# Contrast adjustment on one core: 64 KB rows in three kept buffers, two hardware DMA queues, tiles moved as every second row, sum shared by two engines

## The chip, the cores and the metric

The kernel runs on one core of a Trainium2 chip. The metric is device time in microseconds (us) of one execution; figures are medians of several executions, with their range. A profile covers one execution, and its span is about 2 us shorter than the metric. Runs are marked fast or slow by their time alone. The experiments ran in three batches on different chips, each beside the kernel before, whose medians there were 240.29, 240.23 and 239.88 us; differences of half a microsecond between batches are therefore not resolved.

A packet is one record of the DMA trace, here nearly always one contiguous run of a transfer (also called a row below; 1536 records of 64 KB in the changed kernel), on one of 16 DMA engines. In the trace each transfer ends with 16 packets of 4 bytes, called completion writes below (416 for the 26 transfers of the kernel before), and has 16 semaphore updates; it has landed at the last of these.

## The reference

```python
# x: 16 x 3 x 512 x 512 float32, factor = 1.5
def reference(x, factor):
    mean = np.mean(x, axis=(2, 3), keepdims=True)
    return np.clip(mean + factor * (x - mean), 0, 1).astype(np.float32)
```

There are 48 images of 1 MB. Each must be read in full before its mean is known, and then every pixel is rescaled and clipped. 50.33 MB are read and 50.33 MB written, whatever the kernel does.

## The kernel before

A tile is four images, 4 MB: 32 partitions for each image, 32 KB in each partition, one DMA in and one out. Eleven such tiles are followed by two of two images, so that the last one is small. Five buffers rotate. VectorE sums each partition, a matmul with a block matrix adds the partitions of an image, ScalarE applies `relu(1.5 x + bias)` and VectorE takes the minimum with 1.

```python
TILE_IMGS = [4] * 11 + [2, 2]
X_BUFS = 5
STORE_ENGINE = "gpsimd"
# ... (pools, block matrices, addresses cut)
    for i, N in enumerate(TILE_IMGS):
        FREE = n_pix * N // P                       # 8192 columns for four images
        nc.sync.dma_start(out=xt, in_=src)          # P rows of FREE elements
        nc.vector.tensor_reduce(out=rsum, in_=xt, axis=mybir.AxisListType.X, op=mybir.AluOpType.add)
        nc.tensor.matmul(pbias, blockw[N], rsum, start=True, stop=True)
        nc.scalar.copy(out=bias, in_=pbias)
        nc.scalar.activation(out=xt, in_=xt, func=mybir.ActivationFunctionType.Relu, bias=bias, scale=factor)
        nc.vector.tensor_scalar(out=xt, in0=xt, scalar1=1.0, scalar2=None, op0=mybir.AluOpType.min)
        store_eng.dma_start(out=dst, in_=xt)        # gpsimd: the software queue
```

Of the kernel before, what the change touches and what calls it, by code (L numbers as in the profile page):

```python
# [1 line left out]

# [4 lines left out]


TILE_IMGS = [4] * 11 + [2, 2]  # L10
X_BUFS = 5
STORE_ENGINE = "gpsimd"


@with_exitstack
def kernel(
    ctx: ExitStack,
    tc: tile.TileContext,
    x: bass.AP,
    factor: float,  # L20
    out: bass.AP,
):
    nc = tc.nc
    P = 128

    B, C, H, W = x.shape
    n_img = B * C
    n_pix = H * W

    factor = float(factor)  # L30
    f32 = mybir.dt.float32

    assert sum(TILE_IMGS) == n_img
    NMAX = max(TILE_IMGS)

    x_f = x.rearrange("b c h w -> (b c h w)")
    out_f = out.rearrange("b c h w -> (b c h w)")

    wconst = (1.0 - factor) / float(n_pix)

    consts = ctx.enter_context(tc.tile_pool(name="consts", bufs=1))
    blockw = {}
    for N in sorted(set(TILE_IMGS)):
        wt = consts.tile([P, P], f32, name=f"blockw{N}")
        PPI = P // N
        if N == 1:
            nc.gpsimd.memset(wt, wconst)
        else:
            nc.gpsimd.memset(wt, 0.0)  # L49
            for b in range(N):  # L50
                nc.gpsimd.memset(wt[b * PPI : (b + 1) * PPI, b * PPI : (b + 1) * PPI], wconst)  # L51
        blockw[N] = wt

    xpool = ctx.enter_context(tc.tile_pool(name="xpool", bufs=X_BUFS))
    rpool = ctx.enter_context(tc.tile_pool(name="rpool", bufs=12))
    bpool = ctx.enter_context(tc.tile_pool(name="bpool", bufs=12))
    psum = ctx.enter_context(tc.tile_pool(name="psum", bufs=8, space=bass.MemoryType.PSUM))

    if STORE_ENGINE == "sync":
        store_eng = nc.sync  # L60
    elif STORE_ENGINE == "act":
        store_eng = nc.scalar
    else:
        store_eng = nc.gpsimd

    pix_off = 0
    for i, N in enumerate(TILE_IMGS):
        FREE = n_pix * N // P
        npix_tile = n_pix * N

        xt = xpool.tile([P, NMAX * n_pix // P], f32, name="xt")[:, :FREE]
        src = bass.AP(tensor=x_f.tensor, offset=pix_off, ap=[[FREE, P], [1, FREE]])
        dst = bass.AP(tensor=out_f.tensor, offset=pix_off, ap=[[FREE, P], [1, FREE]])
        nc.sync.dma_start(out=xt, in_=src)  # L74

        rsum = rpool.tile([P, 1], f32)
        nc.vector.tensor_reduce(  # L77
            out=rsum,
            in_=xt,
            axis=mybir.AxisListType.X,  # L80
            op=mybir.AluOpType.add,
        )

        pbias = psum.tile([P, 1], f32)
        nc.tensor.matmul(pbias, blockw[N], rsum, start=True, stop=True)  # L85

        bias = bpool.tile([P, 1], f32)
        nc.scalar.copy(out=bias, in_=pbias)  # L88

        nc.scalar.activation(  # L90
            out=xt,
            in_=xt,
            func=mybir.ActivationFunctionType.Relu,
            bias=bias,
            scale=factor,
        )
        nc.vector.tensor_scalar(  # L97
            out=xt,
            in0=xt,
            scalar1=1.0,  # L100
            scalar2=None,
            op0=mybir.AluOpType.min,
        )
        store_eng.dma_start(out=dst, in_=xt)  # L104

        pix_off += npix_tile


# [1 line left out]
_INS = ['x', 'factor']  # L110
_OUTS = [((16, 3, 512, 512), 'float32')]
#: Inputs that are plain numbers.
_NUMBERS = {'factor': 1.5}


# [26 lines left out]
```

## Time and profile before

| | before |
|---|---|
| time | 240.01 us (239.79 to 240.62) when predicted; 240.19 us with later runs |
| span of the profile | 238.6 us |
| HBM traffic over the span | 422 GB/s |
| busy: VectorE (DVE), ScalarE (ACT) | 66%, 37% |

These are lines of the page of the kernel before. A digit is the busy share of one fortieth of the span in tenths; the GB/s line has the traffic in the same slices.

```profile
span 238.6 us, 238 instructions
...
DVE  0088999999599079459629909917945979742300
ACT  2002966472906601900920650470190095406000
...
DMA  7999999999999999999999999999999999999995
GB/s 269 434 439 439 439 439 352 439 434 439 439 439 439 439 434 434 423 428 412 423 439 439 434 439 439 439 439 439 434 428 426 426 404 428 431 434 439 428 434 214
```

The DMA strip is full from the second slice to the last but one, while both compute engines have gaps. The next view gives the same by stretches, 42 to 196 us and the three stretches of the end: length, then busy us (instructions) of TensorE's matmuls (PE), its weight loads (PEld), VectorE, ScalarE and POOL, then clock, DMA share, GB/s.

```profile
42.00:196.00 154.00, 5.18 (x18) 4.50 (x18) 110.74 (x18) 63.07 (x18) 4.80 (x9) 1.00 1.01 434
196.00:217.00 21.00, 1.12 (x4) 1.01 (x4) 15.47 (x4) 6.39 (x4) 2.99 (x2) 1.00 0.99 421
217.00:225.00 8.00, 0.00 (x0) 0.00 (x0) 2.29 (x1) 3.83 (x2) 0.53 (x1) 1.00 1.05 455
```

From 217 to 225 us the last small tile is still being computed, and the DMA engines are full nonetheless, with stores that had queued up. The groups of instructions price the compute (busy us, mean ns of one, idle before and what ended it):

```profile
L77 DVE TENSOR_REDUCE rsum<-xt 128x1 f32<-128x8192 f32 (+1 forms) x13 | 104.4, 8029 | 61.7 <-DMA xt<-in_x_dram 61.7
L90 ACT ACTIVATE xt<-xt,bias 128x8192 f32<-128x8192 f32 (+1 forms) x13 | 85.8, 6598 | 0.4
L97 DVE TENSOR_SCALAR xt<-xt 128x8192 f32<-128x8192 f32 (+1 forms) x13 | 53.2, 4091 | 5.0 <-ACT xt L90 5.0
```

VectorE waits for loads, 61.7 us in all, not the other way round.

### The profile page before, as it was taken

Reading aid. Unit: us, or ns where it says so; the run is one execution under the profiler, and the core shown is the slowest. Engines: PE = TensorE matmul, PEld = TensorE weight load, DVE = VectorE, ACT = ScalarE, POOL = GpSimd, SP = SyncE. Lnnn points to the kernel's source line nnn. Section 1 sums busy time; section 2 is a strip of 40 time slices with the busy share of each in tenths; the row PEclk is TensorE's granted clock in tenths of the full one; section 3 lists DMA queues with packets and bytes.
Section 4 is the critical chain, followed back from the end, with each engine's and each line's share of the span. In section 5 each row is a group of like instructions: output and inputs, shape, how many; then the busy total and the mean of one; then the engine's idle time right before and its main releaser. Section 6 shows DMA issues by size and latency. Waiting matters only on the chain.

```text
span 238.6 us, 238 instructions
## 1 busy us (share of the span) xinstructions
PE 7.4 (3%) x26; PEld 6.5 (3%) x26; DVE 156.5 (66%) x26; ACT 89.1 (37%) x27; POOL 10.3 (4%) x25
## 2 busy tenths in 40 slices
PE   0000000000000000000000000000000000000000
PEld 0000000000000000000000000000000000000000
DVE  0088999999599079459629909917945979742300
ACT  2002966472906601900920650470190095406000
POOL 2000001000000000000000000000000000500000
DMA  7999999999999999999999999999999999999995
GB/s 269 434 439 439 439 439 352 439 434 439 439 439 439 439 434 434 423 428 412 423 439 439 434 439 439 439 439 439 434 428 426 426 404 428 431 434 439 428 434 214
DMA packets 3744, 100.66 MB, mean 422 GB/s; under 512 B 416, under 2 KB 416, under 8 KB 416
## 3 DMA queue, kind: packets, MB, share of 16 engines
q1 hardware_dynamic: 1872, 50.33, 49.4%
q0 software_dynamic: 1872, 50.33, 49.0%
HBM read 50.33 MB, written 50.33 MB: 422 GB/s over the span
## 4 chain that ended last, share of the span: by engine, by line
issue 38%; DMA 35%; DVE 18%; POOL 2%; POOLq 0%; SPq 0%
DMA xt<-in_x_dram 19%; DMA out_dram<-xt 16%; DVE rsum L77 11%; DVE xt L97 7%; POOL out_dram L104 2%; POOLq L137 0%; SPq L74 0%; POOLq L104 0%
## 5 line engine op out<-in xcount | busy, mean ns | idle before, releaser
L77 DVE TENSOR_REDUCE rsum<-xt 128x1 f32<-128x8192 f32 (+1 forms) x13 | 104.4, 8029 | 61.7 <-DMA xt<-in_x_dram 61.7
L90 ACT ACTIVATE xt<-xt,bias 128x8192 f32<-128x8192 f32 (+1 forms) x13 | 85.8, 6598 | 0.4
L97 DVE TENSOR_SCALAR xt<-xt 128x8192 f32<-128x8192 f32 (+1 forms) x13 | 53.2, 4091 | 5.0 <-ACT xt L90 5.0
L88 ACT COPY bias<-pbias 128x1 f32<-128x1 f32 x13 | 2.1, 160 | 130.6 <-PE pbias L85 130.6
L104 POOL DMA_DIRECT2D out_dram<-xt x13 | 9.0, 692 | 213.0 <-DVE xt L97 212.8
L85 PE MATMUL pbias<-rsum,blockw 128*128 128x1 f32 x26 | 7.4, 355 | 209.5 <-DVE rsum L77 209.5
L85 PEld LDWEIGHTS pbias<-rsum,blockw 128*128 128x128 f32 x26 | 6.5, 311 | 210.3 <-DVE rsum L77 107.1
L88 ACT ACT_TABLE_LOAD x1 | 1.3, 1283 | 0.8 <-PEq L123 0.8
L51 POOL MEMSET blockw<- 32x32 f32 (+1 forms) x6 | 0.8, 128 | 0.2
L49 POOL MEMSET blockw<- 128x128 f32 x2 | 0.3, 205 | 0.3 <-POOLq L123 0.3
L123 POOL MEMSET const-float32-0.0<- 128x1 f32 x1 | 0.1, 104 | 0.2 <-issue 0.2
L123 POOL MEMSET const-bfloat16-1.0<- 128x1 bf16 x1 | 0.1, 113 | 0.0
L123 POOL MEMSET const-uint8-127<- 128x1 uint8 x1 | 0.1, 113 | 0.0
L123 POOL MEMSET const-float32-1.0<- 128x1 f32 x1 | 0.1, 110 | 0.0
## 6 DMA issues: line engine op xcount, KB each, us to landing
xt<-in_x_dram SPq DMA_DIRECT2D x11, 4096.0 KB, 24.6
out_dram<-xt POOLq DMA_DIRECT2D x11, 4096.0 KB, 36.0
xt<-in_x_dram SPq DMA_DIRECT2D x2, 2048.0 KB, 19.5
out_dram<-xt POOLq DMA_DIRECT2D x2, 2048.0 KB, 19.1
```

Of the source, the lines that this page charges most:

```text
L49: nc.gpsimd.memset(wt, 0.0)
L51: nc.gpsimd.memset(wt[b * PPI : (b + 1) * PPI, b * PPI : (b + 1) * PPI], wconst)
L77: nc.vector.tensor_reduce(out=rsum, in_=xt, axis=mybir.AxisListType.X, op=mybir.AluOpType.add,)
L85: nc.tensor.matmul(pbias, blockw[N], rsum, start=True, stop=True)
L88: nc.scalar.copy(out=bias, in_=pbias)
L90: nc.scalar.activation(out=xt, in_=xt, func=mybir.ActivationFunctionType.Relu, bias=bias, scale=factor,)
L97: nc.vector.tensor_scalar(out=xt, in0=xt, scalar1=1.0, scalar2=None, op0=mybir.AluOpType.min,)
L104: store_eng.dma_start(out=dst, in_=xt)
L123: nc = _bacc.Bacc("TRN2", target_bir_lowering=False, num_devices=1)
```

## The change

Its intent is fewer and longer DMA runs (64 KB in each partition), stores on a hardware queue, and a shorter sum because ScalarE takes half of the columns. A tile is now 8 MB, eight images of 16 partitions; there are six tiles in three buffers. Each tile moves in two DMAs, even rows and odd rows, so that each DMA touches partitions all over the array and a reload can begin when half of the old tile is stored.

```diff
-TILE_IMGS = [4] * 11 + [2, 2]
-X_BUFS = 5
-STORE_ENGINE = "gpsimd"
+ROW = 16384        # elements: 64 KB
+BUFS = 3
+HALF = ROW // 2
+CHUNK = 4096
+JUNK = 2048
+PARTS = 2
 ...
+    def dram(ap, t, r):
+        return bass.AP(tensor=ap.tensor, offset=(t * P + r) * ROW, ap=[[PARTS * ROW, P // PARTS], [1, ROW]])
+    def load(t):
+        for r in range(PARTS):
+            nc.sync.dma_start(out=xt[r::PARTS, :], in_=dram(x_f, t, r))
+    def compute(t):
+        nc.vector.tensor_reduce(out=sums[:, 0:1], in_=xt[:, 0:HALF], ...)
+        for j in range(n_act):                       # 4 pieces of the other half
+            a = HALF + j * JUNK
+            nc.scalar.activation(out=junk, in_=xt[:, a : a + JUNK], func=Act.Copy, accum_out=sums[:, 1 + j : 2 + j])
+        for j in range(1 + n_act):
+            nc.tensor.matmul(pbias, blockw, sums[:, j : j + 1], start=j == 0, stop=j == n_act)
+        nc.scalar.copy(out=bias, in_=pbias)
+        for c in range(0, ROW, CHUNK):
+            part = xt[:, c : c + CHUNK]
+            nc.scalar.activation(out=part, in_=part, func=Act.Relu, bias=bias, scale=factor)
+            nc.vector.tensor_scalar(out=part, in0=part, scalar1=1.0, scalar2=None, op0=Alu.min)
+    def store(t):
+        for r in range(PARTS):
+            nc.scalar.dma_start(out=dram(out_f, t, r), in_=xt[r::PARTS, :])
+    with tc.manual_schedule():
+        for t in range(min(BUFS, n_tiles)): load(t)
+        for t in range(n_tiles):
+            compute(t); store(t)
+            if t + BUFS < n_tiles: load(t + BUFS)
```

(Set-up lines, small tiles and the block matrix are cut.)

More of the change, by code (lines that the diff above doesn't have):

```diff
@@ L5 @@
 import concourse.tile as tile
-from concourse import bass_utils, mybir
+from concourse import mybir
 from concourse._compat import with_exitstack
-TILE_IMGS = [4] * 11 + [2, 2]
-X_BUFS = 5
-STORE_ENGINE = "gpsimd"
+P = 128
+ROW = 16384
[4 more added lines that the diff above has]
+PARTS = 2
 @with_exitstack
@@ L23 @@
     nc = tc.nc
-    P = 128
+    f32 = mybir.dt.float32
+    Alu = mybir.AluOpType
+    Act = mybir.ActivationFunctionType
     B, C, H, W = x.shape
-    n_img = B * C
-    n_pix = H * W
+    n_img, n_pix = B * C, H * W
+    ppi = n_pix // ROW
+    per_tile = P // ppi
+    n_tiles = n_img // per_tile
+    assert ppi * ROW == n_pix and per_tile * n_tiles == n_img
     factor = float(factor)
-    f32 = mybir.dt.float32
-    assert sum(TILE_IMGS) == n_img
-    NMAX = max(TILE_IMGS)
+    wconst = (1.0 - factor) / float(n_pix)
@@ L36 @@
     x_f = x.rearrange("b c h w -> (b c h w)")
     out_f = out.rearrange("b c h w -> (b c h w)")
-    wconst = (1.0 - factor) / float(n_pix)
+    def dram(ap, t, r):
+        return bass.AP(
+            tensor=ap.tensor, offset=(t * P + r) * ROW, ap=[[PARTS * ROW, P // PARTS], [1, ROW]]
+        )
     consts = ctx.enter_context(tc.tile_pool(name="consts", bufs=1))
-    blockw = {}
-    for N in sorted(set(TILE_IMGS)):
-        wt = consts.tile([P, P], f32, name=f"blockw{N}")
-        PPI = P // N
-        if N == 1:
-            nc.gpsimd.memset(wt, wconst)
-        else:
-            nc.gpsimd.memset(wt, 0.0)
-            for b in range(N):
-                nc.gpsimd.memset(wt[b * PPI : (b + 1) * PPI, b * PPI : (b + 1) * PPI], wconst)
-        blockw[N] = wt
@@ L54 @@
-    xpool = ctx.enter_context(tc.tile_pool(name="xpool", bufs=X_BUFS))
-    rpool = ctx.enter_context(tc.tile_pool(name="rpool", bufs=12))
-    bpool = ctx.enter_context(tc.tile_pool(name="bpool", bufs=12))
-    psum = ctx.enter_context(tc.tile_pool(name="psum", bufs=8, space=bass.MemoryType.PSUM))
-    if STORE_ENGINE == "sync":
-        store_eng = nc.sync
-    elif STORE_ENGINE == "act":
-        store_eng = nc.scalar
-    else:
-        store_eng = nc.gpsimd
-    pix_off = 0
-    for i, N in enumerate(TILE_IMGS):
-        FREE = n_pix * N // P
-        npix_tile = n_pix * N
-        xt = xpool.tile([P, NMAX * n_pix // P], f32, name="xt")[:, :FREE]
-        src = bass.AP(tensor=x_f.tensor, offset=pix_off, ap=[[FREE, P], [1, FREE]])
-        dst = bass.AP(tensor=out_f.tensor, offset=pix_off, ap=[[FREE, P], [1, FREE]])
-        nc.sync.dma_start(out=xt, in_=src)
-        rsum = rpool.tile([P, 1], f32)
+    xpool = ctx.enter_context(tc.tile_pool(name="xpool", bufs=1))
@@ new lines @@
+    jpool = ctx.enter_context(tc.tile_pool(name="jpool", bufs=1))
+    rpool = ctx.enter_context(tc.tile_pool(name="rpool", bufs=2))
+    bpool = ctx.enter_context(tc.tile_pool(name="bpool", bufs=2))
+    psum = ctx.enter_context(tc.tile_pool(name="psum", bufs=2, space=bass.MemoryType.PSUM))
+    blockw = consts.tile([P, P], f32, name="blockw")
+    nc.gpsimd.memset(blockw, 0.0)
+    for a in range(0, P, 2 * ppi):
+        mid, end = a + ppi, a + 2 * ppi
+        nc.gpsimd.memset(blockw[a:end, mid:end], wconst)
+        nc.gpsimd.memset(blockw[a:mid, mid:end], 0.0)
+        nc.gpsimd.memset(blockw[a:mid, a:mid], wconst)
@@ L77 @@
+    bufs = [xpool.tile([P, ROW], f32, name=f"x{b}") for b in range(BUFS)]
+    def load(t):
+        xt = bufs[t % BUFS]
+        for r in range(PARTS):
+            nc.sync.dma_start(out=xt[r::PARTS, :], in_=dram(x_f, t, r))
+    def compute(t):
+        xt = bufs[t % BUFS]
+        n_act = (ROW - HALF) // JUNK
+        sums = rpool.tile([P, 1 + n_act], f32, name="sums")
         nc.vector.tensor_reduce(
-            out=rsum,
-            in_=xt,
-            axis=mybir.AxisListType.X,
-            op=mybir.AluOpType.add,
-        )
@@ L84 @@
-        pbias = psum.tile([P, 1], f32)
-        nc.tensor.matmul(pbias, blockw[N], rsum, start=True, stop=True)
-        bias = bpool.tile([P, 1], f32)
-        nc.scalar.copy(out=bias, in_=pbias)
-        nc.scalar.activation(
-            out=xt,
-            in_=xt,
-            func=mybir.ActivationFunctionType.Relu,
-            bias=bias,
-            scale=factor,
-        )
-        nc.vector.tensor_scalar(
-            out=xt,
-            in0=xt,
-            scalar1=1.0,
-            scalar2=None,
-            op0=mybir.AluOpType.min,
-        )
@@ L104 @@
-        store_eng.dma_start(out=dst, in_=xt)
-        pix_off += npix_tile
+            out=sums[:, 0:1], in_=xt[:, 0:HALF], axis=mybir.AxisListType.X, op=Alu.add
+        )
+        for j in range(n_act):
+            junk = jpool.tile([P, JUNK], f32, name="junk")
+            a = HALF + j * JUNK
+            nc.scalar.activation(
+                out=junk, in_=xt[:, a : a + JUNK], func=Act.Copy, accum_out=sums[:, 1 + j : 2 + j]
+            )
+        pbias = psum.tile([P, 1], f32, name="pbias")
@@ new lines, in compute @@
+        for j in range(1 + n_act):
+            nc.tensor.matmul(pbias, blockw, sums[:, j : j + 1], start=j == 0, stop=j == n_act)
+        bias = bpool.tile([P, 1], f32, name="bias")
+        nc.scalar.copy(out=bias, in_=pbias)
+        for c in range(0, ROW, CHUNK):
+            part = xt[:, c : c + CHUNK]
+            nc.scalar.activation(out=part, in_=part, func=Act.Relu, bias=bias, scale=factor)
+            nc.vector.tensor_scalar(out=part, in0=part, scalar1=1.0, scalar2=None, op0=Alu.min)
@@ L110 @@
+    def store(t):
+        xt = bufs[t % BUFS]
+        for r in range(PARTS):
+            nc.scalar.dma_start(out=dram(out_f, t, r), in_=xt[r::PARTS, :])
+    with tc.manual_schedule():
+        for t in range(min(BUFS, n_tiles)):
+            load(t)
+        for t in range(n_tiles):
+            compute(t)
+            store(t)
+            if t + BUFS < n_tiles:
+                load(t + BUFS)
 _INS = ['x', 'factor']
```

## The prediction

The sum in this text came to a span of 239 to 240.5 us, about 241.5 us of time. The author's guess gave one chance in five to 255 to 300 us with rows in steps of two.

> **What bounds the kernel now.** The DMA engines. The busy-tenths strip shows DMA at 9 in every slice but the first and last, at 434 to 439 GB/s in most; the windows view gives 434 GB/s and a full DMA share from 62 to 196 us. In the trace's DMA records every full packet is one 32 KB row and mostly takes 1.213 us on one of 16 engines. 100.66 MB is 3072 such rows, so 3072 x 1.213 / 16 = 232.9 us of the 238.6 us span is transfer that no schedule removes. Left are about 6 us: start (first packet at 1.75 us, first 4 MB tile landed at 13.0 instead of 11.4), small dips, and 1.8 us from the last packet to the end. DVE (66% busy) and ACT (37%) are not the bound.
>
> **What changes.** Bytes stay the same. Rows double to 64 KB: a 16 KB row took 0.611 us against 1.213 for 32 KB, so about 0.009 us per packet is fixed; 1536 fewer packets over 16 engines save 0.9 us. Stores leave the software queue of POOL (4.7 us from the first store's issue to its first packet; a hardware load needs 1.0 us). With queues nearly always full, that saves under 1 us.
>
> Added: tiles are 8 MB, six of them, in three buffers. Compute of one tile, from the trace's durations: DVE sum of 8192 columns 8.7 us, with ACT's four 2048-column sums (about 2.0 us each by its slope) beside it; ten fp32 matmul passes instead of two, about 2.5 to 3 us; four Relu pieces of 3.65 us; last min 2.3 us: about 28.5 us landing to store. Each tile needs 38.6 us of transfer, so in the middle compute hides. A half's reload waits only for that half's store.
>
> **The ends decide.** The start is hidden: 24 MB of loads keep DMA busy until about 58 us, while the first tile lands at 22.7 us and its store comes at about 51.5 us. At the end, before has two 2 MB tiles; now the last 8 MB tile lands at about 189 us, computes until about 217, then has 19.3 us of stores. Stores still queued when it lands cover some 23 to 27 us of that, so DMA idles for about 2 to 6 us. A sum with equal shares for both queues gives a span of 239 to 240.5 us, about 241.5 us of time: saved packets against the tail hole.
>
> [...]
>
> **Predicted: 241.5 us, range 237.5 to 253.** Faster by over 2%: 0.03; within 2%: 0.67; slower: 0.30.
>
> **What would show it.** Right: 64 KB packets at about 2.42 us; 434 GB/s from 6 to 200 us; a DMA dip near 210 to 217 us; the chain ending in last-tile compute (sum, matmul, Relu, min) followed by about 20 us of store. Wrong: packets longer than 2.6 us or fewer GB/s in the first 50 us[...]; holes in the middle (three buffers too few[...]); compute per tile over 33 us.

## The result, and the profile after

| | before | after |
|---|---|---|
| time | 240.19 us (239.79 to 240.62) | 246.95 us (245.16 to 249.87) |
| span of the profile | 238.6 us | 244.7 us |
| GB/s over the span | 422 | 411 |

The ratio is 1.0264, with a 95% interval of 1.0221 to 1.0307: slower by 2.6%. A ratio is the mean time of one kernel's fast runs over that of the other's of the same rounds, so it is not quite the ratio of the medians. One of the four runs (249.87 us) counted as slow; the median of the three fast ones is 246.51 us, which is also the profiled run. Differences below are taken from this 246.51.

The same lines of the page for the changed kernel:

```profile
span 244.7 us, 338 instructions
...
DVE  0002925597157933730853550490761192563000
ACT  0002979939895879910859930486970195990000
...
DMA  9797989997979798999998999999999999834995
GB/s 343 343 514 343 514 375 482 407 450 343 514 343 514 343 503 353 503 396 461 418 441 353 503 396 461 418 439 428 439 418 439 428 428 471 386 171 171 514 439 246
```

The see-saw between 343 and 514 is how whole 64 KB packets fall into slices of 6 us; the trace's DMA records, spread over each packet's duration, give 430 to 434 GB/s in nearly every stretch up to 218 us. What is real is the "34" near the end of the DMA strip, with ScalarE at "99" just above it. By stretches:

```profile
60.00:190.00 130.00, 9.14 (x40) 8.79 (x40) 62.67 (x19) 83.42 (x46) 0.00 (x0) 1.00 0.99 428
196.00:217.00 21.00, 2.29 (x10) 2.21 (x10) 12.07 (x4) 17.87 (x13) 0.00 (x0) 1.00 0.95 412
217.00:225.00 8.00, 0.00 (x0) 0.00 (x0) 4.51 (x2) 3.48 (x1) 0.00 (x0) 1.00 0.31 131
```

From 217 to 225 us the DMA share is 0.31, where it was 1.05 before. The chain of waits that ended last shows who holds it up; columns are start, duration and what:

```profile
167.35 27.25 DMA x<-in_x_dram
...
194.72 8.70 DVE sums L82
203.41 0.04 issue
203.46 2.31 PE pbias L93 x10
205.76 0.02 issue
205.79 0.17 ACT bias L95
...
209.59 10.90 ACT x L98 x3
220.52 2.29 DVE x L99
```

The last tile lands at 194.60 us. Its sum, ten matmul passes (the page counts 60 for the 30 matmuls), four clipped pieces and the last minimum run one after another until 222.8 us, and only then can either of its stores be issued. The groups confirm the prices of the single steps (VectorE's sum of half the columns 8.683 us, the pieces 3.696 and 2.294 us, ScalarE's partial sums 1.909 us plus 0.186 us each for reading the accumulator):

```profile
L98 ACT ACTIVATE x<-x,bias 128x4096 f32<-128x4096 f32 x24 | 87.0, 3696 | 0.2
L99 DVE TENSOR_SCALAR x<-x 128x4096 f32<-128x4096 f32 x24 | 55.1, 2294 | 61.5 <-ACT x L98 61.5
L82 DVE TENSOR_REDUCE sums<-x 128x1 f32<-128x8192 f32 x6 | 52.1, 8683 | 54.4 <-DMA x<-in_x_dram 54.4
L88 ACT ACTIVATE junk<-x 128x2048 f32<-128x2048 f32 x24 | 45.8, 1909 | 46.0 <-DMA x<-in_x_dram 38.1
```

To see where the hole comes from, the trace's DMA records were grouped by transfer (this is a calculation from the trace, not a view of the profile; us from the span's start):

```
                          issued   first packet   last packet ends   landed
before  first store        36.06       40.72
before  first reload       61.44       64.94
before  a middle reload   157.19      161.84          180.15         181.72
before  last load         192.35      196.71          210.13         211.71
after   first store        51.35       56.80           72.06
after   first reload       72.53       76.36           94.51          97.27
after   last load         167.35      173.92          191.82         194.60
after   last store but 2  184.71      207.14          218.39         218.74
after   last tile's store 222.84      223.98
after   its second half   223.36      233.71          243.55         243.90
```

The end of the changed kernel adds up exactly: landing 194.60 + 28.24 of compute + 1.14 to the first packet + 19.57 of store + 1.18 to the end = 244.73 us. The stores of earlier tiles had run out at 218.39, so no packet was in flight for 5.59 us. Divided by 16 engines, the packets' times sum to 234.6 us after and 234.5 us before, so nearly all of the 6.1 us by which the span grew is time in which engines stood idle (10.2 us of the span after, 4.1 before). So the loss is mainly that hole, and bytes did not get slower: a 64 KB packet took 2.418 us and a 32 KB packet 1.213 us in the median, 2.444 and 1.221 us in the mean. The saving of 0.9 us that was expected of longer rows does not show.

### The profile page after: what moved, and what is told of

It is laid out like the page before. It is cut to its first block, busy times and chain, and to the rows that moved or that the text cites. A ratio compares the mean times of both kernels' runs of the same rounds, so it can differ in the third digit from the quotient of the medians.

```text
span 244.7 us, 338 instructions
## 1 busy us (share of the span) xinstructions
PE 13.7 (6%) x60; PEld 13.2 (5%) x60; DVE 107.0 (44%) x30; ACT 137.3 (56%) x79; POOL 1.4 (1%) x17
## 4 chain that ended last, share of the span: by engine, by line
DMA 37%; ACT 21%; DVE 16%; another core or an unknown queue 8%; issue 5%; PE 4%; SPq 0%; DVEq 0%
ACT x L98 21%; DMA x<-in_x_dram 20%; DMA out_dram<-x 17%; DVE sums L82 14%; PE pbias L93 4%; DVE x L99 2%; SPq L76 0%; ACT bias L95 0%; DVEq L82 0%
## 5 line engine op out<-in xcount | busy, mean ns | idle before, releaser
L98 ACT ACTIVATE x<-x,bias 128x4096 f32<-128x4096 f32 x24 | 87.0, 3696 | 0.2
L99 DVE TENSOR_SCALAR x<-x 128x4096 f32<-128x4096 f32 x24 | 55.1, 2294 | 61.5 <-ACT x L98 61.5
L82 DVE TENSOR_REDUCE sums<-x 128x1 f32<-128x8192 f32 x6 | 52.1, 8683 | 54.4 <-DMA x<-in_x_dram 54.4
L88 ACT ACTIVATE junk<-x 128x2048 f32<-128x2048 f32 x24 | 45.8, 1909 | 46.0 <-DMA x<-in_x_dram 38.1
L93 PE MATMUL pbias<-sums,blockw 128*128 128x1 f32 x60 | 13.7, 354 | 192.0 <-DVE sums L82 192.0
L93 PEld LDWEIGHTS pbias<-sums,blockw 128*128 128x128 f32 x60 | 13.2, 329 | 192.4 <-DVE sums L82 160.5
L88 ACT ACT_TABLE_LOAD x1 | 1.3, 1283 | 23.1 <-DMA x<-in_x_dram 23.1
L95 ACT COPY bias<-pbias 128x1 f32<-128x1 f32 x6 | 1.0, 159 | 13.8 <-PE pbias L93 13.8
L88 ACT ACTIVATION_READ_ACCUMULATOR junk<-x 128x1 f32 x24 | 4.5, 186 | 0.0
L67 POOL MEMSET blockw<- 16x16 f32 x4 | 0.4, 104 | 0.2
L68 POOL MEMSET blockw<- 16x16 f32 x4 | 0.4, 104 | 0.0
```

What stands on the lines that cost most here:

```text
L67: nc.gpsimd.memset(blockw[a:mid, mid:end], 0.0)
L68: nc.gpsimd.memset(blockw[a:mid, a:mid], wconst)
L82: nc.vector.tensor_reduce(out=sums[:, 0:1], in_=xt[:, 0:HALF], axis=mybir.AxisListType.X, op=Alu.add)
L88: nc.scalar.activation(out=junk, in_=xt[:, a : a + JUNK], func=Act.Copy, accum_out=sums[:, 1 + j : 2 + j])
L93: nc.tensor.matmul(pbias, blockw, sums[:, j : j + 1], start=j == 0, stop=j == n_act)
L98: nc.scalar.activation(out=part, in_=part, func=Act.Relu, bias=bias, scale=factor)
```

## The experiments

Theory: the DMA engines are full throughout, so compute counts only where the store queue runs dry, behind the last tile; and it runs dry there because splitting tiles by rows makes the sum wait for both DMAs and both stores wait for the last column. Rivals: compute in series slows the middle through three buffers; 64 KB runs, 64 partitions in steps of two, or the hardware queue cost something of their own.

### Longer compute in the middle, and at the end

Two kernels change one number: in chosen tiles VectorE sums all columns alone.

```diff
+        cut = ROW if t in (2, 3, 4) else HALF     # first kernel;  t in (5,) in the second
-        n_act = (ROW - HALF) // JUNK
+        n_act = (ROW - cut) // JUNK
-            ... in_=xt[:, 0:HALF]
+            ... in_=xt[:, 0:cut]
```

> The changed kernel, but in tiles 2, 3 and 4 VectorE sums all 16384 columns alone (17.4 us for the sum instead of 8.7, and one matmul instead of five, so compute of these tiles is about 7 us longer). Theory (only the last tile's compute lies on the critical path, because the DMA engines are full until 218 us): no change, 247 us within 1 us. Rival (compute per tile, 28 us in series, delays every store and so every reload in three buffers): three tiles at 7 us, so up to 20 us slower, 255 to 267 us.

> The same lengthening in tile 5, the last, alone. Theory: the hole before the last store grows by the full 7 us, from 5.6 to about 12.5 us, and the time becomes about 253.5 us (252.5 to 255). Rival (the loss is spread over the middle): one tile of six, about 1 us slower.

Lengthening three middle tiles gave 246.86 us (245.66 to 246.98), ratio 1.0267 against the 1.0264 of the changed kernel: nothing. Lengthening the last tile alone gave 253.62 us (251.72 to 254.67), 7.1 us more than the changed kernel. Its timeline shows the sum on one engine and the store that follows:

```profile
193.10 17.22 DVE L83 TENSOR_REDUCE sums<-x 128x1 f32<-128x16384 f32 x1 [10.55 <-DMA x<-in_x_dram]
...
228.06 1.13 ACTq L105 DMA_DIRECT2D out_dram<-x  x2
```

The time without any packet grew from 5.6 to 12.1 us (217.14 to 229.20). In the first kernel the middle tiles did get longer: tile 3 needed 35.1 us from landing to store instead of 28.2. The same lengthening costs nothing in three tiles of the middle and its full size in the last. The rival of a slowed middle falls.

### Column halves instead of every second row

```diff
-            offset=(t * P + r) * ROW, ap=[[PARTS * ROW, P // PARTS], [1, ROW]]
+            offset=t * P * ROW + r * (ROW // PARTS), ap=[[ROW, P], [1, ROW // PARTS]]
-        ... xt[r::PARTS, :]
+        ... xt[:, r * ROW // PARTS : (r + 1) * ROW // PARTS]
```

> The changed kernel with every tile moved in two DMAs of column halves (128 partitions, 32 KB runs) instead of every second row (64 partitions, 64 KB runs); order and bytes per DMA as before. Theory (a landing and a first packet wait behind one or more packets of the other queue): the landing lag in mixed stretches falls from 2.8 to about 1.6 us, the last load ends some 2 us earlier in the store queue's favour, time about 245 us (243.5 to 246). [...] theory: 1.213 us per 32 KB, the same. Rival (long rows save time): slower than 247 us.

It gave 239.54 us (239.48 to 239.68), ratio 0.9974 (0.9956 to 0.9992). That beats the changed kernel by 2.8% and is a quarter of a per cent under the kernel before, which counts as the same; it misses the expectation, which had looked only at waiting behind packets. The timeline of its last tile shows what had been overlooked:

```profile
182.57 8.68 DVE L82 TENSOR_REDUCE sums<-x 128x1 f32<-128x8192 f32 x1
...
195.54 1.91 ACT L88 ACTIVATE junk<-x 128x2048 f32<-128x2048 f32 x1 [15.21 <-DMA x<-in_x_dram]
...
214.18 0.34 ACTq L104 DMA_DIRECT2D out_dram<-x  x1
...
221.38 0.34 ACTq L104 DMA_DIRECT2D out_dram<-x  x1
```

VectorE sums the first half of the columns at 182.6 us, before the second half has landed at 195.52; and the first half is stored at 214.2 us, 7.2 us ahead of the second, although both stores stand after all the work in program order (ScalarE's sequencer issued the DMA at 214.18 us, while its engine was in the third piece until 215.42). The first store needs 18.7 us from the landing instead of 28.2. The hole is gone:

```profile
217.00:225.00 8.00, 0.00 (x0) 0.00 (x0) 3.04 (x2) 2.02 (x1) 0.00 (x0) 1.00 0.99 426
```

But this kernel differs from the changed one in three things at once: the DMAs themselves (32 KB runs, 128 partitions each instead of 64), early sum, early store. The next two separate them.

### Column halves made late again

Both move column halves. In the first, the order of pieces makes the first store wait for the last piece, and VectorE's half of the sum straddles both DMAs. The second has the order of pieces alone.

```diff
-        for c in range(0, ROW, CHUNK):
+        for c in (2 * CHUNK, 3 * CHUNK, 0, CHUNK):                 # both kernels
-            ... in_=xt[:, 0:HALF]
+            ... in_=xt[:, HALF // 2 : HALF // 2 + HALF]            # all-late kernel only
-            a = HALF + j * JUNK
+            a = j * JUNK if j < n_act // 2 else HALF + j * JUNK    # all-late kernel only
```

> Column halves in 32 KB runs as in the third experiment, but made as late as in the changed kernel: VectorE sums the middle half of the columns, so it needs both DMAs, and the pieces are clipped in the order third, fourth, first, second, so that the first store waits for the last piece. From the last landing to the first store 27.5 to 28.5 us as in the changed kernel. Theory A (the gain of columns came from starting the sum and the store early): the hole before the last store returns, 3 to 6 us, time 243.5 to 246. Theory B (the gain came from 32 KB instead of 64 KB runs, or from 128 instead of 64 partitions): time stays at 239.5 to 240.5.

> Column halves, sum started early (VectorE on the half that lands first), but both stores late by the order of pieces. Landing of the second half to first store about 25.8 us. Theory A: about 2.5 us better than the all-late run, 241 to 243, so that the early store accounts for the rest down to 239.5. Theory B: 239.5 to 240.5, no different from the columns run.

All late: 244.61 us (244.41 to 245.54), as its theory A had it, and the stretch without a packet is back, from 217.67 to 222.93. Early sum alone: 243.64 us (243.23 to 244.17), slightly above the 241 to 243 expected, with 2.8 us without a packet (218.70 to 221.54). Early store as well, the run above: 239.54 us. So of the 7.0 us between row halves and column halves, about 4.1 come from the store that starts early, about 1.0 from the sum that starts early, and the rest, about 1.9 by the medians, from moving columns at all; no run separates the shorter runs from the 128 partitions there. The profiled spans put that last part at 0.9 us (244.7 to 243.8), so its size is not well known. Nor do the parts add up in any order: the early store alone, with everything else by rows, brings 5.6 us (next experiment). A piece of the last part can be seen: while the other queue was busy, a load landed 2.8 us after its last packet in the changed kernel (191.82 to 194.60), 1.6 us in the kernels with 32 KB runs (192.19 to 193.84 here, 180.15 to 181.72 before), and 0.3 to 0.5 us with no other queue busy.

### Only the last tile's store by columns

```diff
+            if t == n_tiles - 1:
+                cols = bass.AP(tensor=out_f.tensor, offset=t * P * ROW + r * HALF, ap=[[ROW, P], [1, HALF]])
+                nc.scalar.dma_start(out=cols, in_=xt[:, r * HALF : (r + 1) * HALF])
+            else:
-            nc.scalar.dma_start(out=dram(out_f, t, r), in_=xt[r::PARTS, :])
+                nc.scalar.dma_start(out=dram(out_f, t, r), in_=xt[r::PARTS, :])
```

> The changed kernel in everything but the store of the last tile, which leaves as two column halves instead of every second row. The first of them needs only the first two of four clipped pieces and can be issued about 7 us earlier, at about 215.7 us, before the earlier stores have drained at 218.4. Theory (the whole loss beside the kernel before is the hole at 218 to 224 us): the hole of 5.6 us closes, time 241 to 241.8. Rival (64 KB rows, or hardware queues, cost in the middle too): 244 or more.

It gave 240.90 us (239.36 to 241.13), ratio 1.0012 (0.9973 to 1.0052), the same as before. Of its two stores the first was issued at 216.05 instead of 222.84 us, and no moment without a packet was left after the start. Ten of twelve stores and all loads still move as 64 KB rows of every second partition, on two hardware queues. So those parts cost at most about 1.3 us together beside the kernel before (the interval's upper end, net of whatever the change gains), and one pair of DMA instructions at the end accounts for 5.6 us (246.51 to 240.90), the length of the hole. The strip of this run for comparison:

```profile
span 239.3 us, 339 instructions
...
DMA  9898989897999898989898989898989999998994
```

### Contiguous halves of the rows

```diff
-            offset=(t * P + r) * ROW, ap=[[PARTS * ROW, P // PARTS], [1, ROW]]
+            offset=(t * P + r * P // PARTS) * ROW, ap=[[ROW, P // PARTS], [1, ROW]]
-        ... xt[r::PARTS, :]
+        ... xt[r * P // PARTS : (r + 1) * P // PARTS, :]
```

> The changed kernel with rows 0 to 63 in the first DMA and 64 to 127 in the second, instead of every second row. [...] packets of 64 KB take about 4.8 us in the load-only start, about 217 GB/s, the first tile lands at about 41 us instead of 23 and the time passes 300 us. If the step of two is irrelevant: 2.42 us per packet, 247 us.

It took 390.94 us (380.93 to 391.88). The first tile landed at 44.1 us instead of 23.1, and the load-only start runs at half the rate:

```profile
GB/s 215 215 215 215 215 215 188 168 289 323 256 323 330 242 336 316 256 336 309 269 323 310 303 309 303 309 323 323 316 303 336 343 242 135 47 121 215 222 209 108
```

So the partitions of a single DMA mattered by a factor of two here: 64 neighbouring ones moved at 215 GB/s in this start, 64 in steps of two at 434 GB/s. Why was not shown. The edit also makes each DMA's rows neighbours in HBM, but that is not the reason: one DMA of 128 neighbouring rows (next experiment) ran its load-only start at 434 GB/s. What the prediction feared, slow packets with rows in steps of two, is another pattern, and no run produced it.

### One DMA for a tile

```diff
-PARTS = 2
+PARTS = 1
```

> The changed kernel with one DMA of 128 rows per tile instead of two of every second row. A reload then waits for the store of a whole tile, about 9 to 10 us longer, once per buffer turn; the load queue falls behind and the last tile lands some 2 us later, at about 196 us, with fewer stores left behind it. Theory: 247.5 to 249.5. If the reload by halves was worth nothing: 246.9[...].

It gave 254.73 us (254.10 to 255.95), 5 us worse than the expectation's upper end. A reload then waits for a whole tile's store: the load queue was empty from 66.9 to 86.1 us, the last tile landed at 202.9 us, and 12.5 us passed without a packet (219.43 to 231.92). The strip shows the hole as wide:

```profile
DMA  8979999799989998989979999899899998303994
```

The direction was right and the size was not. The first reload was issued 9.3 us later than in the changed kernel (81.84 against 72.53), as expected, and its first packet waited 4.2 us against 3.8; but of this delay 8.3 us reached the last landing (202.87 against 194.60), where the expectation had let 2 through. While the load queue was empty the stores ran alone, so fewer of them were left to cover the end. Splitting the tile was worth 8.2 us (254.73 against 246.51).

### The stores' queue

```diff
-            nc.scalar.dma_start(out=dram(out_f, t, r), ...)       # changed kernel
+            nc.gpsimd.dma_start(out=dram(out_f, t, r), ...)

-STORE_ENGINE = "gpsimd"                                           # kernel before
+STORE_ENGINE = "act"
```

> The changed kernel with its stores back on the software queue of POOL. In both kernels the first store's first packet came about 5 us after its issue (4.7 software, 5.4 hardware), with the load queue busy, so the kind of queue should matter little; at the end of the kernel, with nothing in flight, the hardware store needed 1.1 us[...]. Theory: 246.5 to 248.5. If the hardware queue itself was the gain or the loss of the change: off by over 2 us either way.

> The kernel before with its stores on the hardware queue of ACT, the one part of the change that costs nothing elsewhere. The DMA engines have under 1.5 us of idle to give back beside the start, so theory: 239.3 to 240.5, at most 0.4 per cent better. If it is over 1 us slower, ACT is held up by waiting for VectorE before each store.

The changed kernel with software-queue stores took 248.52 us (246.72 to 249.24), at the upper edge of the expectation; its profiled span was 244.9 us against 244.7 for the changed kernel. By the ratios (1.0333 against 1.0264, intervals overlapping) the software queue is slower by something between nothing and 3 us; more is not resolved. The expectation allowed the software queue an extra microsecond in the hole; that is not in the trace: the last tile's store needed 1.11 us from issue to first packet, against 1.14 on the hardware queue.

The kernel before with stores on ScalarE's queue took 271.57 us (270.83 to 272.38), 13% slower and far outside the expectation. The queue is not the reason. Before, the scheduler orders the instructions, and it put two or three stores in a row into ScalarE's stream, each of which waits for VectorE's minimum; ScalarE stands still behind them. From the view of waits (who waited for whom: us in total, times, longest):

```profile
ACT bias L88 <- PE pbias L85: 101.9, 6, 29.0
ACT bias L88 <- DVE xt L97: 60.0, 4, 23.0
```

The second line is such a stop; it does not occur before, when POOL did this waiting (212.8 us for VectorE's minimum). Three stretches without a packet, of 2.5, 9.4 and 13.3 us, each end with a store that ScalarE issued late (at 133.59, 198.67 and 247.81 us). This is read from the one trace; no run gave this kernel a fixed order. So, as far as these runs show, the hardware queue and the fixed program order of the change belong together; taking the first without the second costs 31 us.

### Four column quarters

The column kernel with `PARTS = 4`, that is 16 KB runs.

> The changed kernel with four column quarters per tile (128 partitions, 16 KB runs). Starts sum and stores earlier still, and lets the landing lag fall to about 1 us (one packet of 0.61 us plus 0.4), but the packets cost 1.222 instead of 1.213 us per 32 KB, 1.7 us over the kernel. With no hole left to close: 240.5 to 242, between 1 and 2 us slower than two column halves.

It gave 240.41 us (240.07 to 241.11), ratio 1.0017 (0.9983 to 1.0051), just under the 240.5 to 242 expected. A 16 KB packet took 0.611 us, the rate fell from 433 to 431 GB/s, and there was no hole left to close. Loads landed 0.97 us after their last packet beside a busy queue, as expected. Two halves have the lowest time found, though the two intervals touch.

## Why the prediction was right or wrong

The measured 246.95 us lies inside the stated range of 237.5 to 253, and 5.5 us above the 241.5 that was named. The mechanism named, a hole at the end behind the last tile's compute, is what came; its size and so the sign of the result were missed, and it was the width of the range that held the number. The outcome held likeliest, within 2%, did not come; the kernel is 2.6% slower, to which 0.30 had been given.

- **What bounds the kernel:** right. Three middle tiles lengthened by about 7 us each changed nothing, and a kernel without a hole returns to 239.5 to 241 us.
- **"The ends decide":** right, and shown twice: the last tile's compute counts in full, and storing that one tile by columns gives the time back. Compute from landing to store was put at about 28.5 us and was 28.2.
- **"The last 8 MB tile lands at about 189 us":** this is the step that failed. It landed at 194.6, and everything behind it is added to that. The prediction's text has 1.0 us from issue to first packet, as for the very first load, when nothing else was in flight, and no lag of a landing. In a queue that has run empty beside a busy one it was 5.4 us for the first store and 3.8 us for the first reload, which began at 76.4 us. The landing of the last load came 2.8 us after its last packet. The trace before showed both: 3.5 us for the first reload, 4.7 for the first store (which the prediction put down to the software queue) and 1.6 us of landing lag. A third part is the mean packet, where the prediction counted every row at the median: the 1232 packets done when the last load ended took 2.449 us in the mean, not 2.418, which is 2.4 us over 16 engines. An estimate puts the three together: a replay of the two queues with equal shares (in the changed kernel loads and stores each moved 214 GB/s from 80 to 140 us), a small calculation and not a run, lands the last tile at 187.7 us with 1.0 us to a first packet, a lag of 0.35 us and packets of 2.418 us, and at 194.9 us with 5.45 and 3.83 us, 2.78 us and 2.444 us as measured. No run changed one of the three alone.
- **"DMA idles for about 2 to 6 us":** it was 5.6 us, inside the stretch but at its far end; the span of 239 to 240.5 us fits only its near end. The dip came at 218.4 to 224.0 us, not at 210 to 217.
- **"Save 0.9 us" by 64 KB rows:** not seen; packets summed to 234.6 us against 234.5, and the mean 64 KB packet took about twice the mean 32 KB one (2.444 and 1.221 us).
- **The hardware queue "saves under 1 us":** not contradicted. The runs leave anything from nothing to 3 us in the changed kernel.
- **The risk with rows in steps of two, one chance in five of 255 to 300 us:** it did not come about; 64 rows in steps of two ran at 434 GB/s. Contiguous rows were slow (391 us), which is another pattern.
- **What it did not see at all:** the split by rows is what makes the tail long. A row split gives no column to start on early. The prediction treated 28.5 us as the price of an 8 MB tile, when the same tile in column halves needs 18.7 us to its first store.

The landing lag is explained by the traces. It fits one packet of the other queue at three sizes (0.36 + 2.42 = 2.78 us, 0.36 + 1.21 = 1.57 us, 0.36 + 0.61 = 0.97 us), and the queues take turns in the traces: of the 1064 data packets that start from 100 to 180 us in the kernel before, 932 start where packets of the other queue alone end (12 ns apart at most), and 391 of 528 in the changed kernel. The records of the changed kernel's last load show the waiting itself: all 16 completion writes start 2.41 us after a last data packet of the load (from 188.42 to 190.83 us for the first, from 191.82 to 194.23 us for the last), each at the moment at which a packet of the store queue ends. For the last load of the kernel before it is 1.21 us (from 208.88 to 210.09 us for the first), again up to the end of a store packet. For the very first load, with no store in flight, they follow their data at once, within 0.01 us in the changed kernel.

Left open: why a first packet takes 3.5 to 5.5 us beside a busy queue in a queue that has run empty (the first stores and first reloads of the two kernels), against 1.14 us with nothing in flight, and how the gain of about 1 to 2 us from moving columns divides between the landing lag and the rest. Of the first store (56.80 us on), too, all 16 first packets start as a packet of the other queue ends, but the wait shrinks far less than the rows do: it was 5.4 us beside 64 KB rows, 4.3 beside 32 KB and 4.0 beside 16 KB.

## What to carry to other kernels

Here the DMA engines were full, and compute was free until the queues ran dry (7 us more in each of three middle tiles cost nothing, in the last tile 7.1 us). In such a kernel look first at what the last tile still has to do after its landing, and how much stored-up traffic covers it. Split a tile's DMAs along the axis along which compute is split, so that work can begin on the first piece and its store can leave before the last (18.7 us from landing to first store here); a split along the other axis kept every wait at full length (28.2 us). In a schedule sum, take issue-to-packet and landing times from a stretch where both queues are busy (3.8 to 5.4 us and 2.8 us in the changed kernel), not from the quiet start (1.0 and 0.35 us in the kernel before).
